# Two of twelve output pairs stored in rows of 4 KB, and a second half-store cut into 92, 4 and 32 partitions

## The chip, the core and the metric

The kernel runs on one NeuronCore of a Trainium2 chip. The core has a matrix engine (TensorE, PE in the profile, with its weight loads as PEld), a vector engine (VectorE, DVE), a scalar engine (ScalarE, ACT), a general engine (GpSimd, POOL), and an engine that here only issues transfers (SyncE, SP). Transfers between the chip's main memory (HBM) and the on-chip memory (SBUF) run on 16 DMA engines. The metric is the device time of one execution in microseconds (us). The kernel before takes 128.76 us, the median of three runs (128.62 to 128.79).

## The reference

Inputs Q, K and V have the shape (8, 12, 512, 64) in float32: 96 heads of 512 tokens with 64 features. For each head:

```
Q_norm = Q / (norm of Q over the 512 tokens)          # a norm per feature
K_norm = K / (norm of K over the 512 tokens)
attn   = einsum('bhnd,bhne->bhde', Q_norm, K_norm)    # 64 x 64, contracted over tokens
attn   = softmax(attn, last axis)
out    = einsum('bhnd,bhde->bhne', V, attn)           # 512 x 64
```

Three inputs of 12.58 MB are read and one output of 12.58 MB is written. Nothing is read twice.

## The kernel before

Four heads make a unit (`HU = 4`), so there are `U = 24` units. Two units make a pair, `S = 12` pairs `s`; two pairs make one of `W = 6` loads of V.

**The way to the attention matrix.** Rows of Q and K come in by DMA (`load_qk`, line 172), are cast to bf16 next to each other (`cast_qk`, 209), and one chain of matmuls per head accumulates all products of features (`grams`, 221). The diagonal gives the norms (`squares`, `sums`, `powers`), the off-diagonal block gives the logits, and `exps` (278) and `normalise` (285) leave `ab[s]`: for each of four head positions a 128 x 128 block-diagonal bf16 matrix that holds the attention of the head of unit 0 and of the head of unit 1.

**The way to the output.** V comes in rows of 32 tokens, 8 KB each (`load_v`, 189), is cast (`cast_v`) and transposed on TensorE (`vtrans`, 295) to `vt[w]` of shape [128, 8 j, 128 x, 4 c]: features of two units on the partitions, and for each row x (16 rows a head) its token 8c + j. `outs` (310) then multiplies. A piece `x` of pair `s` is `(i, k) = divmod(x, 2)`: `i` picks two of four head positions, `k` picks four of eight `j`. Each piece is 8 matmuls: for each `j` and each of two heads, 64 columns of `vt` (16 rows times 4 `c`) are the weights, the 128 columns of `ab` stream through, and the result lands on 64 partitions of the PSUM tile `po` (two buffers). `ocopy` (321) copies `po` to the SBUF tile `so[s, i]` of shape [128, 2 r, 8 j, 64], on ACT or, in the last pairs, on DVE. So a partition of `so[s, i]` holds, for each of the two units `r`, eight neighbouring tokens of one head: 512 floats, which are a run of 2 KB in the output. `sop` (147) has 13 buffers for these tiles (`NB`, 140), so a tile waits for the store of the tile 13 before it.

**The stores.** `store` (198) writes a tile of 512 KB as one DMA of 256 rows of 2 KB (line 207). Two stores are not like that. The store of pair 9, `i = 1` (`FEW`, 122) is four DMAs: its half `r = 0` goes in parts of 92, 4 and 32 partitions (line 204), its half `r = 1` whole (line 205). The last store, of pair 11, `i = 1`, is cut by `j` into two DMAs of 256 rows of 1 KB (planned at 457 and 458), the first of which needs one piece less.

**What sets the order.** Nothing is scheduled by hand or by the framework's scheduler: `Order` (the class at the top) is a small list scheduler that runs while the kernel is being written out. Every step is a `piece` with a cost for each engine it may run on, what it must come after, and a rank; `run` picks the next step, and each engine's instructions stand in that order. The planner also counts PE instructions (`size`, 353; `pause`, 44) to allow for instruction fetches. All DMAs but two (the first K loads, on ACT's queue) are issued by SP, in one queue. SP issues a DMA only when the instructions before it in its queue are through and the data or the buffer is there.

SP's last instructions, in order: fourteen stores of 512 KB (pairs 2 to 9; the fourteenth is pair 9, `i = 0`), the four DMAs of pair 9, `i = 1`, then three stores of 512 KB (pair 10 twice, pair 11 `i = 0`) and two of 256 KB (pair 11, `i = 1`). Below, the stores of pairs 10 and 11 are called the last four stores.

Of the kernel before, what the change touches and what calls it, by code (L numbers as in the profile page):

```python
# [8 lines left out]
F32 = mybir.dt.float32  # L9
# [4 lines left out]
D = 64  # L14
T = 16
HU = 4
J = T // 2
# [85 lines left out]
def kernel(  # L103
# [7 lines left out]
    nc = tc.nc  # L111
# [3 lines left out]
    S = U // 2  # L115
# [4 lines left out]
    HELD, UNTIL = ("lk", 1, 1), ("cq", 0, 1)  # L120
    BOTH = S - 8
    FEW = (S - 3, 1)

# [8 lines left out]

    Of = out.rearrange("b h n d -> (b h n d)").rearrange(
        "(w r e i p x) -> w e i p r x", r=2, e=2, i=2, p=128, x=J * D)

    ctx.enter_context(tc.manual_schedule())

    NB = dict(qk=3, v=3, vb=2, qkb=2, vt=2, so=13, sm=2, ab=4)  # L140
    const = ctx.enter_context(tc.tile_pool(name="const", bufs=1))
    qp = ctx.enter_context(tc.tile_pool(name="qp", bufs=NB["qk"]))
    vp = ctx.enter_context(tc.tile_pool(name="vp", bufs=NB["v"]))
    vbp = ctx.enter_context(tc.tile_pool(name="vbp", bufs=NB["vb"]))
    qkp = ctx.enter_context(tc.tile_pool(name="qkp", bufs=NB["qkb"]))
    vtp = ctx.enter_context(tc.tile_pool(name="vtp", bufs=NB["vt"]))
    sop = ctx.enter_context(tc.tile_pool(name="sop", bufs=NB["so"]))
    small = ctx.enter_context(tc.tile_pool(name="small", bufs=NB["sm"]))
    ps_v = ctx.enter_context(tc.tile_pool(name="ps_v", bufs=1, space=bass.MemoryType.PSUM))
    ps_l = ctx.enter_context(tc.tile_pool(name="ps_l", bufs=1, space=bass.MemoryType.PSUM))  # L150
# [11 lines left out]
    qk32, v32, vb, qkb, gram, scr, kq, n2, r8, kqs, rq, lg, ex, ab, vps, vt, po, so = ({} for _ in range(18))  # L162

    def copy(eng, o, i):
        if eng == "ACT":
            nc.scalar.copy(o, i)  # L166
        elif eng == "DVE":
            nc.vector.tensor_copy(o, i)  # L168
        else:
            nc.gpsimd.tensor_scalar(out=o, in0=i, scalar1=1.0, scalar2=0.0, op0=ALU.mult, op1=ALU.add)  # L170
# [24 lines left out]
        else:  # L195
            nc.sync.dma_start(out=o[:, c], in_=i[:, c])

    def store(s, i, k=None):
        rows = slice(None) if k is None else slice(k * (J // 2), (k + 1) * (J // 2))
        o = Of[s // 2, s % 2, i].rearrange("p r (j d) -> p r j d", d=D)  # L200
        if (s, i) == FEW:

            for a, b in ((0, 92), (92, 96), (96, 128)):
                nc.sync.dma_start(out=o[a:b, 0], in_=so[s, i][a:b, 0])
            nc.sync.dma_start(out=o[:, 1], in_=so[s, i][:, 1])
            return
        nc.sync.dma_start(out=o[:, :, rows], in_=so[s, i][:, :, rows])

    def cast_qk(u, x):
        s, r = divmod(u, 2)  # L210
# [99 lines left out]
    def outs(s, x):  # L310
        i, k = divmod(x, 2)
        w, half = divmod(s, 2)
        po[s, x] = ps_o.tile([128, J // 2, 2, D], F32, name="po")
        for j in range(J // 2):
            for e in range(2):
                h = 2 * i + e
                x16 = slice(16 * (4 * half + h), 16 * (4 * half + h + 1))
                v = vt[w][:, k * (J // 2) + j, x16, :].rearrange("p x c -> p (x c)")
                nc.tensor.matmul(po[s, x][e * D:(e + 1) * D, j].rearrange("p r d -> p (r d)"), v, ab[s][:, h, :])  # L319

    def ocopy(eng, s, x):
        i, k = divmod(x, 2)
        if k == 0:
            so[s, i] = sop.tile([128, 2, J, D], F32, name="so")
        o = so[s, i][:, :, k * (J // 2):(k + 1) * (J // 2)].rearrange("p r j d -> p j r d")
        copy(eng, o, po[s, x])


# [2 lines left out]
    for r in range(2):  # L331
# [7 lines left out]
        name=nc.get_next_instruction_name(), engine=mybir.EngineType.Activation, ins=[], outs=[], act_func_set_id=LN_EXP))  # L339
# [8 lines left out]
    for i in range(NB["ab"]):  # L348
        a = const.tile([128, HU, 2 * D], BF16, name=f"ab{i}")
# [3 lines left out]
    def size(key):  # L353
        if key[0] == "gr" and key[1] >= WIDE:
            return 64
        return 8 if key[0] == "vt" and key[-1] is not None else {"gr": 128, "lg": 8, "vt": 16, "ou": 16}[key[0]]

    plan = Order(size)
    X = 1.29
    R = dict(cq=2.5, gr=2.471, sq=0.756, kq=1, rd=3.457, pw=3.5, sc=1, rq=1.9, lg=5, ex=1.1, nm=2.545, cv=1.165, vt=0.9, vc=1.1, ou=2, oc=0.9)  # L360
    BIAS = dict(sc=-0.6, kq=5, cv=1, vc=-0.3, oc=0.6)
    QK_PACE, V_FROM, V_PACE, ST_LAG = 0.631, 0.0377, 0.7486, 1.5133

    def v_at(v):
        return V_FROM + V_PACE * v / U

    def piece(key, engines, after, behind, rank, fn, *args):
        if key[0] in ("cv", "vc", "oc", "kq", "sc"):
            plan.add(key, engines, after, behind, rank, lambda eng: fn(eng, *args))
        else:  # L370
            plan.add(key, engines, after, behind, rank, lambda eng: fn(*args))

    def back(kind, i, n, *rest):
        return (kind, i - n, *rest) if i - n >= 0 else None
# [5 lines left out]
    def loaded(x, s, r):  # L380
        return ("l" + "qk"[x], s, r if len(parts(s)) == 2 else None)

    last = None
    for s in range(S):
        free = [back("cq", 2 * s + r, 2 * NB["qk"], x) for r in range(2) for x in range(2)]
        for r in parts(s):
            at = QK_PACE * (2 * s + (r or 0)) / U
            for x in range(2):
                key = loaded(x, s, r)
                piece(key, {"DMA": X if r is not None else 2 * X}, free, [last], at, load_qk, s, x, r)  # L390
                last = key
    for u in range(U):
        s, r = divmod(u, 2)
# [17 lines left out]
    def turns(w):  # L411
        return [(q, f) for q in range(4) for f in ((0, 1) if w == W - 1 and q >= TAIL else (None,))]

    last, turned = None, None
    for w in range(W):
        both = 2 * w >= BOTH
        for r in range(2):
            halves = (0, 1) if (w, r) == (W - 1, 1) else (None,)
            n = 2 * w + r - NB["v"]
            for c in halves:  # L420
                free = [("cv", n // 2, n % 2, h) for h in range(2)] if n >= 0 else []
                piece(("lv", w, r, c), {"DMA": X if c is not None else 2 * X}, free, [last], v_at(4 * w + 2 * r + (c or 0)), load_v, w, r, c)
                last = ("lv", w, r, c)
            for c in range(2):
                free = [("vt", w - NB["vb"], *t) for t in turns(w - NB["vb"])] if w >= NB["vb"] else []
                piece(("cv", w, r, c), {"POOL": 1.15, "DVE": (0.72, BIAS["cv"])} if both else {"POOL": 1.15},
                      [("lv", w, r, c if len(halves) == 2 else None)] + free, [("cv", w, r, 0)] if c else [], R["cv"] + 0.01 * (4 * w + 2 * r + c), cast_v, w, r, c)
        for n, (q, f) in enumerate(turns(w)):
            if f is None:
                before = turns(w)[n - 1] if n else turns(w - 1)[-1] if w else None  # L430
                wait = [("vc", w if n else w - 1, *before)] if before else []
            else:
                wait = [("kq", S - 1)] + ([("vc", w, *turns(w)[n - 4])] if n >= 4 and turns(w)[n - 4][1] is not None else [])
# [6 lines left out]
            free = [("ou", 2 * (w - NB["vt"]) + e, x) for e in range(2) for x in range(4)] if w >= NB["vt"] else []  # L440
            piece(("vc", w, q, f), copies, [("vt", w, q, f)] + free, [("vc", w, *turns(w)[n - 1])] if n else [], R["vc"] + 0.02 * w, vcopy, w, q, f)
    for s in range(S):
        for x in range(4):
            i, k = divmod(x, 2)
            n = 4 * s + x - 2
            wait = [("oc", n // 4, n % 4)] if n >= 0 else []
            order = [("ou", s, x - 1) if x else back("ou", s, 1, 3)]
            piece(("ou", s, x), {"PE": 0.5}, [("vc", s // 2, *t) for t in turns(s // 2) if t[0] // 2 == k] + [("nm", s)] + wait, order, R["ou"] + 0.01 * s, outs, s, x)
            n = 2 * s + i - NB["so"]
            free = [("st", n // 2, n % 2)] if k == 0 and n >= 0 else []  # L450
            order = [("oc", s, x - 1) if x else back("oc", s, 1, 3)]
            piece(("oc", s, x), {"ACT": 0.6, "DVE": (0.68, BIAS["oc"])} if s >= BOTH else {"ACT": 0.6}, [("ou", s, x)] + free, order, R["oc"] + 0.01 * s, ocopy, s, x)
        for i in range(2):
            order = [("st", s, 0) if i else back("st", s, 1, 1)]
            if (s, i) == (S - 1, 1):

                piece(("sh", s, i), {"DMA": 0.67}, [("oc", s, 2)], order, v_at(2 * s + i) + ST_LAG, store, s, i, 0)
                piece(("st", s, i), {"DMA": 0.67}, [("oc", s, 3)], [("sh", s, i)], v_at(2 * s + i) + ST_LAG, store, s, i, 1)
            else:
                piece(("st", s, i), {"DMA": X}, [("oc", s, 2 * i), ("oc", s, 2 * i + 1)], order, v_at(2 * s + i) + ST_LAG, store, s, i)  # L460

    ahead = [loaded(x, 0, r) for r in range(2) for x in range(2)]
    held, passed = [], False
# [40 lines left out]
```

## Time and profile before

| what | value |
|---|---|
| median of three runs | 128.76 us (128.62 to 128.79) |
| span of the profiled execution, first to last instruction | 126.98 us |
| the median less this span: what lies around it | 1.78 us |
| DMA: bytes, mean rate | 50.64 MB, 399 GB/s |
| DMA queue 1, share of 16 engines over the span | 96.4% |
| busy share PE, PEld, DVE, ACT, POOL | 61%, 50%, 73%, 57%, 29% |
| last copy of an output tile to SBUF ends | 115.07 us |
| last DMA packet ends | 125.73 us |

The profile is of one execution; its times run from the span's start. The page gives the share of each engine, the span in 40 slices with the DMA rate, the queues, and the issues with their median time from issue to landing. A DMA is cut into packets, here one for each contiguous run in HBM (1, 2, 4 or 8 KB), and on each DMA engine that it uses it ends with a 4-byte packet that counts up a semaphore. So the trace holds, for each DMA, one landing event for each DMA engine that took part, and the DMA has landed when all have come. The windows view gives, for any stretch of the span, the busy time of each engine, the DMA share and the rate. A DMA share a little over 1 is full: records of neighbouring packets overlap by some nanoseconds.

### The profile page before, as it was taken

To read this page: it belongs to the slowest core of one execution; us is meant where nothing else is said; L and a number is where in the kernel's file an instruction comes from. 1 tells how busy PE (TensorE), PEld (TensorE's weight loads), DVE (VectorE), ACT (ScalarE), POOL (GpSimd) and SP (SyncE) were. 2 spreads that over 40 slices of the span, in tenths; PEclk is the share of its full clock that TensorE was granted. 3 is DMA by queue.
4 is the path that set the end of the run, shared out by engine and by line. 5 is a ranking of instruction groups with operands and counts; after the bars stand their busy time and mean duration, and the time that the engine had idled before them with its cause. 6 is when DMAs were issued, how large, how long until landed. Compare 5 with 4: busy or idle time off the path is not lost.

```text
span 127.0 us, 4887 instructions
## 1 busy us (share of the span) xinstructions
PE 77.7 (61%) x2128; PEld 62.9 (50%) x2128; DVE 92.8 (73%) x141; ACT 72.5 (57%) x220; POOL 36.6 (29%) x40
## 2 busy tenths in 40 slices
PE   0065384894844679858594879566797869680000
PEld 0054372773633568647482668445585748460000
DVE  3354749859899899999885898999999799820000
ACT  4000441569877077786692786794829969972000
POOL 4006307300906903033065212213453361200000
PEclk9999999999998555999958967998559995955555
DMA  4999999999999999999999999999999999999993
GB/s 114 415 434 410 430 410 418 417 437 403 425 426 415 410 419 421 405 415 426 430 410 413 415 421 427 412 419 428 401 413 410 403 402 406 401 405 408 405 366 106
DMA packets 15629, 50.64 MB, mean 399 GB/s; under 512 B 1144, under 2 KB 1656, under 8 KB 14200
## 3 DMA queue, kind: packets, MB, share of 16 engines
q1 hardware_dynamic: 15320, 49.29, 96.4%
q10 hardware_dynamic: 288, 1.05, 2.1%
q8 instruction: 16, 0.26, 0.7%
q14 instruction: 5, 0.04, 0.1%
HBM read 37.75 MB, written 12.58 MB: 396 GB/s over the span
## 4 chain that ended last, share of the span: by engine, by line
DVE 39%; DMA 21%; PE 13%; ACT 11%; issue 4%; POOL 2%; DVEq 0%; SPq 0%; POOLq 0%; ACTq 0%
DMA qk<-in_Q_dram 21%; DVE qkb L213 15%; PE gram L233 9%; DVE scr L240 7%; DVE ab L291 6%; ACT vt L166 4%; DVE vb L168 4%; ACT ex L282 3%; ACT so L166 3%; PE vps L302 3%; DVE n L252 2%; DVE vt L168 2%; DVE so L168 2%; PE po L319 1%; ACT kq L166 1%
## 5 line engine op out<-in xcount | busy, mean ns | idle before, releaser
L233 PE MATMUL gram<-qkb 32*128 32x128 bf16 (+1 forms) x1504 | 35.5, 257 | 23.1 <-DVE qkb L213 9.9
L233 PEld LDWEIGHTS <-qkb 32*128 32x128 bf16 (+1 forms) x1504 | 29.9, 114 | 27.7 <-DVE qkb L213 12.7
L213 DVE CAST qkb<-qk 128x1024 bf16<-128x1024 f32 x48 | 36.4, 780 | 8.5 <-DMA qk<-in_Q_dram 6.9
L170 POOL TENSOR_SCALAR vb<-v 128x1024 bf16<-128x1024 f32 x19 | 21.2, 1129 | 45.5 <-DMA v<-in_V_dram 32.0
L166 ACT COPY so<-po 128x512 f32<-128x512 f32 x45 | 25.0, 593 | 5.2 <-PE po L319 5.0
L166 ACT COPY vt<-vps 128x1024 bf16<-128x1024 bf16 (+1 forms) x18 | 17.8, 989 | 17.4 <-PE vps L302 17.3
L302 PE MATMUL vps<-identb,vb 128*128 128x128 bf16 x192 | 20.2, 262 | 5.8 <-POOL vb L170 3.7
L319 PE MATMUL po<-ab,vt 128*64 128x128 bf16 x384 | 19.3, 242 | 5.2 <-issue 2.7
L263 POOL TENSOR_TENSOR kqs<-kq,r 64x512 f32<-64x512 f32 x12 | 14.0, 1164 | 25.8 <-ACT r L259 13.4
L240 DVE SCALAR_TENSOR_TENSOR scr<-gram,eye 64x512 f32<-64x512 f32 x24 | 16.5, 687 | 4.4 <-PE gram L233 4.1
L302 PEld LDWEIGHTS <-vb 128*128 128x128 bf16 x192 | 14.7, 117 | 10.0 <-POOL vb L170 5.1
L319 PEld LDWEIGHTS <-vt 128*64 128x64 bf16 x384 | 13.8, 121 | 9.2 <-issue 4.6
L282 ACT ACTIVATE ex<-lg,rq 128x64 f32<-128x64 f32 x48 | 14.5, 322 | 2.8 <-PE lg L276 2.7
L166 ACT COPY kq<-gram 64x512 f32<-64x512 f32 x12 | 7.0, 581 | 13.5 <-DVE scr L240 13.4
L291 DVE TENSOR_TENSOR ab<-ex,rinv 64x256 bf16<-64x256 f32 x24 | 13.9, 579 | 0.6
L282 ACT ACTIVATION_READ_ACCUMULATOR ex<-lg,rq 128x1 f32 x48 | 10.2, 213 | 0.0
L168 DVE CAST vb<-v 128x1024 bf16<-128x1024 f32 x5 | 7.6, 1527 | 1.2 <-DMA v<-in_V_dram 1.2
L252 DVE TENSOR_REDUCE n<-scr 128x8 f32<-128x512 f32 x12 | 8.1, 679 | 0.1
L276 PE MATMUL lg<-eye,kqs 64*128 64x64 f32 x48 | 6.4, 259 | 2.6 <-issue 1.5
L168 DVE COPY vt<-vps 128x1024 bf16<-128x1024 bf16 (+1 forms) x8 | 7.9, 1019 | 0.1
L276 PEld LDWEIGHTS lg<-eye,kqs 64*128 64x128 f32 x48 | 4.5, 156 | 4.4 <-issue 2.0
L288 DVE RECIPROCAL rinv<-esum 128x4 f32<-128x4 f32 x12 | 2.1, 171 | 2.8 <-ACT ex L282 2.8
(17 smaller groups left out, 16.0 us busy)
## 6 DMA issues: line engine op xcount, KB each, us to landing
v<-in_V_dram SPq DMA_DIRECT2D x11, 1024.0 KB, 17.1
out_dram<-so SPq DMA_DIRECT2D x22, 512.0 KB, 10.2
qk<-in_Q_dram SPq DMA_DIRECT2D x8, 1024.0 KB, 17.4
qk<-in_K_dram SPq DMA_DIRECT2D x8, 1024.0 KB, 17.1
qk<-in_Q_dram SPq DMA_DIRECT2D x8, 512.0 KB, 12.2
qk<-in_K_dram SPq DMA_DIRECT2D x6, 512.0 KB, 12.5
qk<-in_K_dram ACTq DMA_DIRECT2D x2, 512.0 KB, 7.3
v<-in_V_dram SPq DMA_DIRECT2D x2, 512.0 KB
```

What stands on the lines that cost most here:

```text
L166: nc.scalar.copy(o, i)
L168: nc.vector.tensor_copy(o, i)
L170: nc.gpsimd.tensor_scalar(out=o, in0=i, scalar1=1.0, scalar2=0.0, op0=ALU.mult, op1=ALU.add)
L213: nc.vector.tensor_copy(qkb[u][:, :, x * D:(x + 1) * D], qk32[s][:, x, r])
L233: nc.tensor.matmul(gram[s][:, h, r, 0], x, x, start=(t == 0), stop=(t == (T if u < WIDE else J) - 1))
L240: nc.vector.scalar_tensor_tensor(out=scr[s][half], in0=gram[s][half, :, :, 0, half].rearrange("p h r d -> p (h r) d"), scalar=1e-20, in1=e ...
L263: (nc.vector if eng == "DVE" else nc.gpsimd).tensor_tensor(out=kqs[s][HI], in0=kq[s][HI], in1=r8[s][HI, :, None].to_broadcast([D, 2 * HU, ...
L276: nc.tensor.transpose(l[:, h, :], kqs[s][HI, 2 * h:2 * h + 2].rearrange("p r d -> p (r d)"), eye2[HI])
L282: nc.scalar.activation(e[:, h, :], lg[s][:, h, :], AF.Exp, scale=rq[s][:, h:h + 1], accum_out=z[:, h:h + 1])
L291: nc.vector.tensor_tensor(out=a[half, :, half], in0=e[half], in1=ri[half, :, None].to_broadcast([D, HU, D]), op=ALU.mult,)
L302: nc.tensor.transpose(ps[:, c, n, :], vb[w][:, J * c + j].rearrange("p r d -> p (r d)"), identb)
L319: nc.tensor.matmul(po[s, x][e * D:(e + 1) * D, j].rearrange("p r d -> p (r d)"), v, ab[s][:, h, :])
```

## The change

Three things change, and the plan is computed anew with them.

1. Pairs 10 and 11 (`s >= LONG`, `LONG = S - 2`) are multiplied and stored in another layout. In `outs`, `i` now picks two of the four `c` (every second column), and all four heads go side by side: 16 matmuls a piece in place of 8, each with 32 weight columns in place of 64, each landing on 32 partitions. The 128 streamed columns stay. A partition then holds, for each unit, 16 neighbouring tokens of one head, a run of 4 KB. One tile `so[s]` of [128, 2, 16, 64] a pair (pool `slp`, two buffers) takes all four pieces. Its two stores are the two units, each 128 rows of 4 KB, and each waits for all four pieces.
2. The store of pair 9, `i = 1` goes in parts of 92, 4 and 32 partitions for both halves `r`: six DMAs in place of four.
3. The last store is no longer cut in two. `sop` has 12 buffers in place of 13, and the planner's costs and counts follow (0.9 for a piece of 16 matmuls, 32 instructions, a store at 1.23).

```
-    NB = dict(qk=3, v=3, vb=2, qkb=2, vt=2, so=13, sm=2, ab=4)
+    NB = dict(qk=3, v=3, vb=2, qkb=2, vt=2, so=12, sm=2, ab=4)
+    Ol = out.rearrange("b h n d -> (b h n d)").rearrange("(w r e p x) -> w e p r x", r=2, e=2, p=128, x=T * D)
+    slp = ctx.enter_context(tc.tile_pool(name="slp", bufs=S - LONG))
...
-    def store(s, i, k=None):
-        rows = slice(None) if k is None else slice(k * (J // 2), (k + 1) * (J // 2))
-        o = Of[s // 2, s % 2, i].rearrange("p r (j d) -> p r j d", d=D)
-        if (s, i) == FEW:
-
-            for a, b in ((0, 92), (92, 96), (96, 128)):
-                nc.sync.dma_start(out=o[a:b, 0], in_=so[s, i][a:b, 0])
-            nc.sync.dma_start(out=o[:, 1], in_=so[s, i][:, 1])
-            return
-        nc.sync.dma_start(out=o[:, :, rows], in_=so[s, i][:, :, rows])
+    def store(s, i):
+        if s >= LONG:
+            o, t = Ol[s // 2, s % 2][:, i], so[s][:, i].rearrange("p t d -> p (t d)")
...
+        else:
+            o, t = Of[s // 2, s % 2, i], so[s, i].rearrange("p r j d -> p r (j d)")
+            if (s, i) == FEW:
+                for r in range(2):
+                    for a, b in ((0, 92), (92, 96), (96, 128)):
+                        nc.sync.dma_start(out=o[a:b, r], in_=t[a:b, r])
+                return
+        nc.sync.dma_start(out=o, in_=t)
...
-            for e in range(2):
-                h = 2 * i + e
+            for e in range(HU if s >= LONG else 2):
+                h = e if s >= LONG else 2 * i + e
...
-                v = vt[w][:, k * (J // 2) + j, x16, :].rearrange("p x c -> p (x c)")
-                nc.tensor.matmul(po[s, x][e * D:(e + 1) * D, j].rearrange("p r d -> p (r d)"), v, ab[s][:, h, :])
+                v = vt[w][:, k * (J // 2) + j, x16, slice(i, None, 2) if s >= LONG else slice(None)].rearrange("p x c -> p (x c)")
+                n = 32 if s >= LONG else D
+                nc.tensor.matmul(po[s, x][e * n:(e + 1) * n, j].rearrange("p r d -> p (r d)"), v, ab[s][:, h, :])
...
-            if (s, i) == (S - 1, 1):
-
-                piece(("sh", s, i), {"DMA": 0.67}, [("oc", s, 2)], order, v_at(2 * s + i) + ST_LAG, store, s, i, 0)
-                piece(("st", s, i), {"DMA": 0.67}, [("oc", s, 3)], [("sh", s, i)], v_at(2 * s + i) + ST_LAG, store, s, i, 1)
-            else:
-                piece(("st", s, i), {"DMA": X}, [("oc", s, 2 * i), ("oc", s, 2 * i + 1)], order, v_at(2 * s + i) + ST_LAG, store, s, i)
+            done = range(4) if s >= LONG else (2 * i, 2 * i + 1)
+            piece(("st", s, i), {"DMA": X - (0.06 if s >= LONG else 0)}, [("oc", s, x) for x in done], order, v_at(2 * s + i) + ST_LAG, store, s, i)
```

The new plan moves little. SP's queue is the same up to the 92-partition part; then come 92, 4, 32, 92, 4, 32 partitions and four stores of 128 rows of 4 KB. PE's order is the same, with 64 matmuls and 64 weight loads more in the pieces of pairs 10 and 11. ACT makes two output copies of pair 7 after the four exponentials that stood behind them, and one of pair 8 after two small activations that stood behind it; one copy of pair 10 goes from DVE to ACT. POOL's order is the same.

More of the change, by code (lines that the diff above doesn't have):

```diff
@@ L122 @@
     FEW = (S - 3, 1)
+    LONG = S - 2
     Qu = Q.rearrange("b h (p t) d -> (b h p) (t d)", t=T).rearrange("(w r e p) x -> w e p r x", r=2, e=2, p=128)
@@ L196, in load_v @@
             nc.sync.dma_start(out=o[:, c], in_=i[:, c])
-    def store(s, i, k=None):
-        rows = slice(None) if k is None else slice(k * (J // 2), (k + 1) * (J // 2))
-        o = Of[s // 2, s % 2, i].rearrange("p r (j d) -> p r j d", d=D)
-        if (s, i) == FEW:
-            for a, b in ((0, 92), (92, 96), (96, 128)):
-                nc.sync.dma_start(out=o[a:b, 0], in_=so[s, i][a:b, 0])
-            nc.sync.dma_start(out=o[:, 1], in_=so[s, i][:, 1])
-            return
-        nc.sync.dma_start(out=o[:, :, rows], in_=so[s, i][:, :, rows])
+    def store(s, i):
+        if s >= LONG:
+            o, t = Ol[s // 2, s % 2][:, i], so[s][:, i].rearrange("p t d -> p (t d)")
+            if s == FEW[0]:
+                for a, b in ((0, 92), (92, 96), (96, 128)):
+                    nc.sync.dma_start(out=o[a:b], in_=t[a:b])
+                return
[3 more added lines that the diff above has]
+                for r in range(2):
+                    for a, b in ((0, 92), (92, 96), (96, 128)):
+                        nc.sync.dma_start(out=o[a:b, r], in_=t[a:b, r])
+                return
+        nc.sync.dma_start(out=o, in_=t)
     def cast_qk(u, x):
@@ L314, in outs @@
         for j in range(J // 2):
-            for e in range(2):
-                h = 2 * i + e
+            for e in range(HU if s >= LONG else 2):
+                h = e if s >= LONG else 2 * i + e
                 x16 = slice(16 * (4 * half + h), 16 * (4 * half + h + 1))
-                v = vt[w][:, k * (J // 2) + j, x16, :].rearrange("p x c -> p (x c)")
-                nc.tensor.matmul(po[s, x][e * D:(e + 1) * D, j].rearrange("p r d -> p (r d)"), v, ab[s][:, h, :])
+                v = vt[w][:, k * (J // 2) + j, x16, slice(i, None, 2) if s >= LONG else slice(None)].rearrange("p x c -> p (x c)")
+                n = 32 if s >= LONG else D
+                nc.tensor.matmul(po[s, x][e * n:(e + 1) * n, j].rearrange("p r d -> p (r d)"), v, ab[s][:, h, :])
     def ocopy(eng, s, x):
         i, k = divmod(x, 2)
-        if k == 0:
+        if s >= LONG and x == 0:
+            so[s] = slp.tile([128, 2, T, D], F32, name="sl")
+        elif s < LONG and k == 0:
             so[s, i] = sop.tile([128, 2, J, D], F32, name="so")
-        o = so[s, i][:, :, k * (J // 2):(k + 1) * (J // 2)].rearrange("p r j d -> p j r d")
+        o, at = (so[s], i * J) if s >= LONG else (so[s, i], 0)
+        o = o[:, :, at + k * (J // 2):at + (k + 1) * (J // 2)].rearrange("p r j d -> p j r d")
         copy(eng, o, po[s, x])
@@ L355, in size @@
             return 64
-        return 8 if key[0] == "vt" and key[-1] is not None else {"gr": 128, "lg": 8, "vt": 16, "ou": 16}[key[0]]
+        return 8 if key[0] == "vt" and key[-1] is not None else {"gr": 128, "lg": 8, "vt": 16, "ou": 32 if key[0] == "ou" and key[1] >= LONG else 16}[key[0]]
     plan = Order(size)
@@ L447 @@
             order = [("ou", s, x - 1) if x else back("ou", s, 1, 3)]
-            piece(("ou", s, x), {"PE": 0.5}, [("vc", s // 2, *t) for t in turns(s // 2) if t[0] // 2 == k] + [("nm", s)] + wait, order, R["ou"] + 0.01 * s, outs, s, x)
+            piece(("ou", s, x), {"PE": 0.9 if s >= LONG else 0.5}, [("vc", s // 2, *t) for t in turns(s // 2) if t[0] // 2 == k] + [("nm", s)] + wait, order, R["ou"] + 0.01 * s, outs, s, x)
             n = 2 * s + i - NB["so"]
-            free = [("st", n // 2, n % 2)] if k == 0 and n >= 0 else []
+            free = [("st", n // 2, n % 2)] if k == 0 and n >= 0 and s < LONG else []
             order = [("oc", s, x - 1) if x else back("oc", s, 1, 3)]
```

## The prediction

> **What bounds the kernel.** I read the page first. Its 40 slices show the DMA engines full from the second slice to the last but one; DVE, the busiest compute engine, has 73%. So the sum of transfers sets the length, if they never run dry. The windows view of the end shows how they stop (columns that matter: DMA share and GB/s, last two; PE clock before them):
>
> ```profile
> DMA  4999999999999999999999999999999999999993
> GB/s 114 415 434 410 430 410 418 417 437 403 425 426 415 410 419 421 405 415 426 430 410 413 415 421 427 412 419 428 401 413 410 403 402 406 401 405 408 405 366 106
> DMA packets 15629, 50.64 MB, mean 399 GB/s; under 512 B 1144, under 2 KB 1656, under 8 KB 14200
> ```
> ```profile
> 112.00:116.00 4.00, 2.24 (x32) 1.77 (x32) 0.00 (x0) 2.59 (x5) 0.00 (x0) 0.50 1.05 406
> ...
> 120.00:122.00 2.00, 0.00 (x0) 0.00 (x0) 0.00 (x0) 0.00 (x0) 0.00 (x0) 0.50 1.06 407
> 122.00:122.50 0.50, 0.00 (x0) 0.00 (x0) 0.00 (x0) 0.00 (x0) 0.00 (x0) 0.50 0.98 371
> 122.50:123.00 0.50, 0.00 (x0) 0.00 (x0) 0.00 (x0) 0.00 (x0) 0.00 (x0) 0.50 0.87 336
> ...
> 124.50:125.00 0.50, 0.00 (x0) 0.00 (x0) 0.00 (x0) 0.00 (x0) 0.00 (x0) 0.50 0.65 229
> 125.00:125.25 0.25, 0.00 (x0) 0.00 (x0) 0.00 (x0) 0.00 (x0) 0.00 (x0) 0.50 0.17 57
> 125.25:125.50 0.25, 0.00 (x0) 0.00 (x0) 0.00 (x0) 0.00 (x0) 0.00 (x0) 0.50 0.07 25
> 125.50:126.00 0.50, 0.00 (x0) 0.00 (x0) 0.00 (x0) 0.00 (x0) 0.00 (x0) 0.50 0.03 10
> ```
>
> All computing ends at 115; then 16 full DMA engines drain what SP has queued. They do not stop together: from 122.0 some are idle, at 122.5 to 123.0 a share of 0.87 of 1.05 is 13 engines, and after 125.25 one of sixteen (0.07) works alone until 125.73. The kernel ends with its slowest DMA engine, so two things count: the work in the queue, and how it is spread.
>
> **How the work is spread.** Each store's landing is up to sixteen semaphore events, one an engine. From the trace's events, in us:
>
> ```
> pair 9, i=0, whole    116.44 116.52 116.85 117.00 117.10 117.44 118.09 118.09 119.11 119.21 119.25 119.29 119.32 119.34 119.51 119.52
> 92 partitions, r=0    118.70 118.95 119.30 119.94
>  4 partitions, r=0    118.88 119.12 119.48 120.12
> 32 partitions, r=0    116.65 116.69 117.18 118.28 119.06 119.30 119.32 119.39 119.44 119.47 119.50 119.55 119.67 119.68 119.69 120.30
> last store, 2nd half  122.48 122.69 123.03 124.00 124.81 125.07 125.13 125.25 125.28 125.31 125.34 125.37 125.41 125.53 125.54 126.05
> ```
>
> Eight engines run 2.7 to 3.1 us behind the first, eight are ahead. The parts of 92 and of 4 partitions run on four engines only. The page agrees: section 6 lists 73 DMAs; 71 x 16 + 2 x 4 = 1144, its count of packets under 512 B. So the four do 23 + 1 + 2 = 26 rows of that half and the other twelve 2, where a whole half gives 8 to each. In the trace's packets a 2 KB row takes 84 ns and the next starts 80 ns after it (16 x 2048 B / 80 ns = 410 GB/s, the rows above). 23 rows are 1.85 us, so the four are those that landed the whole store at 118.70 - 1.85 = 116.85, 117.10, 117.44 and 118.09. They follow on: 118.70, 118.88, 119.06 for the first of them, 119.94, 120.12, 120.30 for the last. After it nothing is uneven, and the last rows show the same four at 124.81, 125.07, 125.41 and 126.05: 5.75 us behind their 32-partition parts each. So **one of the four is already the last engine of all**, 0.51 us behind the last of the twelve (125.54).
>
> **The change, part by part.**
>
> *The second half in parts.* Each of the four gets 26 rows and 3 completion packets (6 ns each by the packets) where it had 8 and 1: 18 x 80 + 2 x 6 = +1.45 us. Each of the twelve gets 2 rows for 8: -0.48 us. The slowest is one of the four, so +1.45.
>
> *Rows of 4 KB.* An engine's share of the last four stores (in five DMAs) was 3 x (16 x 80 + 6) + 2 x (16 x 42.5 + 6) = 5.23 us (1 KB rows: 42.5 ns from start to start). Now it is 4 x (8 x 155 + 6) = 4.98 us. The 155 ns is the pitch of the loads' 4 KB rows (packets of 159 ns); a store with such rows is not in this trace. Bounds: two 2 KB rows, 160 ns, for the least gain, which leaves 0.09 us; half of an 8 KB row's 305 ns for the most, 0.33 us. I take 155, its own size: **-0.25 us**, on all sixteen.
>
> *The last store whole.* That gain is in the sum. It now waits for all four pieces in place of two, and so do the others of the last four; see the cover below.
>
> *Two DMAs more on SP.* SP's row of issues has one every 1.28 us from 92.8 on, paced by landings: eight DMA semaphores go round, so a store is issued when the eighth before it has landed (the 92-partition part at 110.63, after a landing at 110.57). The six parts take the slots at 110.6, 111.8, 113.1, 114.4, 115.75 and 117.05; the four last stores get 118.3, 119.6, then, once 92 and 4 have landed, 120.05 and about 120.5. The slowest of the four ends its 32-partition packets of the first half at 119.85 (landed 120.30), so it reaches the first of them at 119.85 + 2.10 = 121.95 and the third at 124.4, so nothing is short there. The eight late engines reach the first at about 119.5, an issue is 1.0 us from its first packet (first issue 0.74, first packet 1.75), so they may idle some tenths, and stay ahead of the four.
>
> The Trainium skill bears on this ("DMA: Bandwidth & Descriptors", Measured, and Rules for kernel authors): it gives about 2.0 us fixed a DMA (for a software-made one) and says that under 64 KB one pays mostly overhead. By that the two added DMAs would cost up to 4 us. The trace disagrees: the 8 KB part landed 0.18 us after the 92-partition part on each of its engines, and the share stays at 1.05 around it, as the queue is full. I take nothing.
>
> *PE, ACT, buffers.* 64 matmuls and weight loads come on top, after 109.7. In the stretch 112 to 116, at half clock, 32 matmuls take 2.24 us, 70 ns each; a 32-column form is not in the trace, so from no gain of time by narrower weights (70) down to half of it (35, the same piece time as now): the eight pieces take 4.5 to 9.0 us. With 12 buffers, pair 8's second tile waits for the store that lands at 102.81, where its first copy ran at 100.9; ACT's exponentials behind it come 0.6 us later, so PE starts at 110.3 and ends by 119.3, the last copy (0.59) by 119.9. The third of the last four stores, whose slot is 120.05, just doesn't wait. The cover: the slowest DMA engine needs it at 124.4, so computing could be 3 us later still before the end moves.
>
> *More instructions.* Queue 8 shows 16 instruction fetches of 16 KB; two times eight engines each fell 1.3 to 1.6 us behind the rest, in the landings, where one came. 128 more PE instructions may bring a seventeenth. On one of the eight late ones it costs nothing: they will be 2.4 us ahead of the last (126.05 + 1.45 against 125.54 - 0.48).
>
> **Sum.** +1.45 - 0.25 = +1.20 us on the last DMA engine: the last packet at 126.93 for 125.73, the span 128.18 for 126.98. With the 1.78 us around it, 129.96, that is the median 128.76 + 1.20. With the bounds of the 4 KB rows 129.88 to 130.12. The lag of the slowest of the four grew by 0.6 us between 104 and 113 (1.02 to 1.65 behind the first). Without that, before would end with the twelve (125.54) and after with the four at 125.41 + 1.20: +1.07. So 129.8 to 130.2 for this case.
>
> **Rivals.**
>
> *Other engines take the second half's parts, or the four are really further ahead* (faster). If the second 92 and 4 fell on four early engines of the twelve (116.44 to 118.09), these would end at most at 124.00 + 1.20 = 125.20, and the former four gain 0.48 + 0.25: 128.03. The same comes out if, in an execution without the profiler, the four lead by 1.9 us more than here. For it: the early ones have the room. Against: 92 and 4 of the first half hit the same four, and nothing in the queue shows a choice. The page named above (Why a DMA increments its semaphore by 16) says that such a transfer takes the lowest-numbered engines, always the same; that speaks against it too. Chance 0.14.
>
> *The four lead by about 1.2 us more than here, so that overload and relief cancel*: 128.6 to 129.0. Chance 0.08.
>
> *Late data* (slower): PE's last pieces, held by a fetch or a wait beyond the cover, move the last two stores. It decides from an issue at 123.4; a fetch's spacing of 6 us on top of 119.9 would be 125.9, 2.5 us past that: 132.5. Against: the fetch before lies 6 us and more back. Chance 0.04.
>
> **How the numbers follow.** Four overloaded engines 0.74, at 129.96. A measurement can tell about 0.2% (0.26 us) from no change. Slower 0.74 + 0.04 = 0.78, same 0.08, faster 0.14. The range takes the forecast's own bounds and reaches to the cancelling case: 128.6 to 130.4, which leaves out the two ends, 0.18.
>
> **What would show it.** Right: over the last microsecond the share falls to four engines (0.25) and then to one; the two 92-partition parts land on the same four; last stores' packets at 159 ns; computing over by 120. Wrong on the spread: all engines stop within half a microsecond. Wrong on the cover: a stretch before 122 with a share well under 1.

## The result, and the profile after

The changed kernel takes 130.34 us, the median of four runs (130.18 to 130.54), against 128.72 us (128.62 to 128.79) before: 1.62 us more. The ratio on record is 1.0129, 95% interval 1.0116 to 1.0143; it is taken from all runs, here and below, and is not exactly the quotient of the two medians (1.0126). The forecast was 129.96 us. The profiled execution has a span of 128.42 us, 1.43 us more than before, and its last DMA packet ends at 127.09 us, 1.36 us later.

From the page after: the packets, the two queues that matter, and the issues of the stores (KB each, then the median us from issue to landing).

```profile
DMA  3999999999999999999999999999999999999791
GB/s 114 410 433 413 427 410 419 420 431 406 434 424 412 407 424 419 401 413 431 429 411 409 422 416 421 424 422 410 407 413 406 405 401 405 401 405 344 285 419 79
DMA packets 14854, 50.66 MB, mean 394 GB/s; under 512 B 1136, under 2 KB 1136, under 8 KB 13424
...
q8 instruction: 17, 0.28, 0.8%
...
out_dram<-so SPq DMA_DIRECT2D x19, 512.0 KB, 11.5
...
out_dram<-sl SPq DMA_DIRECT2D x4, 512.0 KB, 3.9
```

Of before, for comparison:

```profile
q8 instruction: 16, 0.26, 0.7%
...
out_dram<-so SPq DMA_DIRECT2D x22, 512.0 KB, 10.2
```

Two slices near the end now hold 344 and 285 GB/s where before held 408 and 405, and the last slice but one is full again. The packets fell from 15629 to 14854, above all because the stores of pairs 10 and 11 now have 512 rows where they had 1280. Queue 8 has a seventeenth instruction fetch. The last four stores land 3.9 us after their issue, where a store took 10.2 us before: they no longer stand in a full queue.

The windows view of the same stretch (last three columns: PE clock, DMA share, GB/s):

```profile
112.00:116.00 4.00, 3.06 (x96) 1.97 (x95) 0.58 (x2) 3.72 (x7) 0.00 (x0) 0.70 1.05 405
116.00:118.00 2.00, 0.00 (x0) 0.00 (x0) 0.00 (x0) 0.15 (x1) 0.00 (x0) 0.50 0.89 339
118.00:119.00 1.00, 0.00 (x0) 0.00 (x0) 0.00 (x0) 0.00 (x0) 0.00 (x0) 0.50 0.83 317
119.00:120.00 1.00, 0.00 (x0) 0.00 (x0) 0.00 (x0) 0.00 (x0) 0.00 (x0) 0.50 0.61 205
120.00:121.00 1.00, 0.00 (x0) 0.00 (x0) 0.00 (x0) 0.00 (x0) 0.00 (x0) 0.50 0.58 234
121.00:122.00 1.00, 0.00 (x0) 0.00 (x0) 0.00 (x0) 0.00 (x0) 0.00 (x0) 0.50 1.04 424
...
125.50:126.00 0.50, 0.00 (x0) 0.00 (x0) 0.00 (x0) 0.00 (x0) 0.00 (x0) 0.50 0.49 197
126.00:126.50 0.50, 0.00 (x0) 0.00 (x0) 0.00 (x0) 0.00 (x0) 0.00 (x0) 0.50 0.12 49
126.50:127.00 0.50, 0.00 (x0) 0.00 (x0) 0.00 (x0) 0.00 (x0) 0.00 (x0) 0.50 0.06 25
```

There are two things to see. At the end, from 126.0, a share of 0.12 is two of sixteen engines, then one: the overload. But before that, from 116 to 121, engines are idle: a share of about 0.6 where 1.05 is full, between 119 and 121, is nine engines at work and seven idle on average. The waits of SP's queue say for what (us in total, times, longest):

```profile
SPq L215 <- DMA out_dram<-so: 8.5, 12, 0.9
SPq L213 <- DMA out_dram<-so: 7.1, 6, 2.6
```

Line 213 issues the six parts, and one of them waited 2.6 us for an older store's landing. By SP's instructions the parts went out at 110.74, 111.98, 113.26, 114.54, 115.83 and 118.72, the last four stores at 119.80, 121.00, 121.46 and 121.91. The sixth part was held until the store of pair 8, i = 0, had landed on its last engine, at 118.70. Fifteen engines had landed it by 117.1; the sixteenth was busy with the seventeenth fetch, which queue 8's packet shows from 116.69 for 0.95 us. In the landing events one late engine goes from 3.3 to 4.9 us behind the first at this store; why it loses 1.6 us by a packet of 0.95 us is not shown. The next two issues waited for the same engine: 119.80 follows its landing at 119.74, and 121.00 the one at 120.99.

The landings that answer to those shown of before:

```
92 partitions, r=0    118.71 119.01 119.48 120.08
92 partitions, r=1    120.81 121.12 121.58 122.18
32 partitions, r=1, last one on the slowest of the four   122.56
last store            126.00 126.03 126.03 126.05 126.05 126.06 126.06 126.08 126.09 126.09 126.11 126.16 126.24 126.35 126.81 127.41
```

The same spacing in both 92-partition rows, 2.10 us apart, shows that the same four engines took both. By their steps from the first of the last four stores (122.30, 122.61, 123.07, 123.67) they end at 126.05, 126.35, 126.81 and 127.41. Of the other twelve, eleven end together at 126.00 to 126.16, because they had stood idle for the same late issues; the twelfth, at 126.24, is the engine of the fetch, which those issues had waited for.

### The profile page after: what moved, and what is told of

It reads as the page before. It is cut to its first block, busy times and chain, and to the rows that moved or that the text cites. A ratio compares the mean times of both kernels' runs of the same rounds, so it can differ in the third digit from the quotient of the medians.

```text
span 128.4 us, 5010 instructions
## 1 busy us (share of the span) xinstructions
PE 78.0 (61%) x2192; PEld 63.0 (49%) x2192; DVE 92.5 (72%) x140; ACT 73.0 (57%) x221; POOL 36.4 (28%) x40
## 2 busy tenths in 40 slices
DMA packets 14854, 50.66 MB, mean 394 GB/s; under 512 B 1136, under 2 KB 1136, under 8 KB 13424
## 3 DMA queue, kind: packets, MB, share of 16 engines
q10 hardware_dynamic: 288, 1.05, 2.1%
## 4 chain that ended last, share of the span: by engine, by line
DVE 30%; DMA 20%; PE 19%; ACT 14%; issue 7%; SPq 0%; DVEq 0%; ACTq 0%
DMA qk<-in_Q_dram 20%; DVE qkb L221 14%; PE gram L241 13%; DVE scr L248 7%; DVE ab L299 5%; ACT ex L290 4%; PE po L328 3%; ACT vt L169 3%; ACT sl L169 3%; PE vps L310 2%; ACT so L169 2%; DVE n L260 1%; ACT kq L169 1%; DVE vb L171 1%; PE lg L284 1%
## 5 line engine op out<-in xcount | busy, mean ns | idle before, releaser
L241 PE MATMUL gram<-qkb 32*128 32x128 bf16 (+1 forms) x1504 | 37.6, 262 | 23.8 <-DVE qkb L221 8.6
L241 PEld LDWEIGHTS <-qkb 32*128 32x128 bf16 (+1 forms) x1504 | 31.4, 117 | 28.8 <-DVE qkb L221 11.2
L221 DVE CAST qkb<-qk 128x1024 bf16<-128x1024 f32 x48 | 39.0, 836 | 8.0 <-DMA qk<-in_Q_dram 6.2
L169 ACT COPY so<-po 128x512 f32<-128x512 f32 x38 | 21.2, 592 | 7.6 <-PE po L328 6.0
L328 PE MATMUL po<-ab,vt 128*64 128x128 bf16 (+1 forms) x448 | 20.5, 243 | 7.2 <-issue 2.6
L310 PE MATMUL vps<-identb,vb 128*128 128x128 bf16 x192 | 17.8, 243 | 4.4 <-POOL vb L173 1.8
L328 PEld LDWEIGHTS <-vt 128*64 128x64 bf16 (+1 forms) x448 | 14.0, 116 | 12.0 <-issue 6.7
L310 PEld LDWEIGHTS <-vb 128*128 128x128 bf16 x192 | 13.3, 109 | 7.7 <-issue 3.1
L290 ACT ACTIVATION_READ_ACCUMULATOR ex<-lg,rq 128x1 f32 x48 | 10.2, 212 | 0.0
L171 DVE CAST vb<-v 128x1024 bf16<-128x1024 f32 x5 | 5.0, 998 | 0.1
L169 ACT COPY sl<-po 128x512 f32<-128x512 f32 x8 | 4.5, 596 | 0.3
```

Of the source, the lines that this page charges most:

```text
L221: nc.vector.tensor_copy(qkb[u][:, :, x * D:(x + 1) * D], qk32[s][:, x, r])
L241: nc.tensor.matmul(gram[s][:, h, r, 0], x, x, start=(t == 0), stop=(t == (T if u < WIDE else J) - 1))
L290: nc.scalar.activation(e[:, h, :], lg[s][:, h, :], AF.Exp, scale=rq[s][:, h:h + 1], accum_out=z[:, h:h + 1])
L310: nc.tensor.transpose(ps[:, c, n, :], vb[w][:, J * c + j].rearrange("p r d -> p (r d)"), identb)
L328: nc.tensor.matmul(po[s, x][e * n:(e + 1) * n, j].rearrange("p r d -> p (r d)"), v, ab[s][:, h, :])
```

## The experiments

Two theories stood after the result, and both could hold at once. **O**: the rows on four engines set the end, as forecast. **F**: the seventeenth fetch sets it, by the engine that it holds up and by SP's wait for that engine. The first four runs pull them apart; run 5 completes the picture, and the rest look at the gain that was to be had. Runs 1 to 4 were timed beside the kernel before on one chip (its median there 128.67 us), runs 5 to 8 on another (128.64 us); each ratio is to the kernel before of its own group.

**1. `long_one_half`**: as changed, but the second half whole.

```
-                for r in range(2):
-                    for a, b in ((0, 92), (92, 96), (96, 128)):
-                        nc.sync.dma_start(out=o[a:b, r], in_=t[a:b, r])
+                for a, b in ((0, 92), (92, 96), (96, 128)):
+                    nc.sync.dma_start(out=o[a:b, 0], in_=t[a:b, 0])
+                nc.sync.dma_start(out=o[:, 1], in_=t[:, 1])
                 return
```

> The changed kernel with the second half of pair 9's store whole again (one DMA of 128 rows), the rest as changed, with its 128 additional PE instructions. Theory O (the time is set by the rows that the two narrow parts of each half put on four DMA engines; the seventeenth instruction fetch is covered): the four lose 1.45 us of rows and end at 127.09 - 1.45 = 125.64, so 130.3 - 1.45 = 128.9 us or, against before, about the same. Theory F (the seventeenth fetch of 16 KB, which in the changed kernel's trace runs from 116.69 and puts the store of pair 8, i = 0, 1.6 us back on one engine, sets the end by itself): that engine has 0.17 + 0.65 + 4.98 us left after its landing of pair 9, i = 0 (120.99, packets some 0.4 earlier) and ends near 126.4, so about 129.5 us. Both give a gain over the changed kernel; they differ by 0.6 us.

Measured: 129.35 us against 128.67 before, ratio 1.0048 (1.0033 to 1.0064). So the second half in parts costs about 1.0 us of the 1.62, and something is left. The end of its windows view:

```profile
124.00:125.00 1.00, 0.00 (x0) 0.00 (x0) 0.00 (x0) 0.00 (x0) 0.00 (x0) 0.50 0.58 238
125.00:125.50 0.50, 0.00 (x0) 0.00 (x0) 0.00 (x0) 0.00 (x0) 0.00 (x0) 0.50 0.14 57
125.50:126.00 0.50, 0.00 (x0) 0.00 (x0) 0.00 (x0) 0.00 (x0) 0.00 (x0) 0.50 0.06 25
126.00:126.50 0.50, 0.00 (x0) 0.00 (x0) 0.00 (x0) 0.00 (x0) 0.00 (x0) 0.50 0.04 16
```

One engine works alone for over half a microsecond, until 126.38. It is not one of the four: the slowest of those lands the last store at 125.88, this one at 126.72. It is the engine that was 3.1 us behind the first at pair 7's last store and 4.6 us at pair 8's first. Theory F's figure for its end was 126.4. Here O alone fails.

**2. `more_matmuls`**: the kernel before, each matmul of the pieces of pairs 10 and 11 issued twice into the same place.

```
-                nc.tensor.matmul(po[s, x][e * D:(e + 1) * D, j].rearrange("p r d -> p (r d)"), v, ab[s][:, h, :])
+                for _ in range(2 if s >= S - 2 else 1):
+                    nc.tensor.matmul(po[s, x][e * D:(e + 1) * D, j].rearrange("p r d -> p (r d)"), v, ab[s][:, h, :])
```

> The kernel before with every matmul of the output pieces of pairs 10 and 11 issued twice into the same place (the second writes the same numbers), so 64 matmuls and 64 weight loads more, as in the change; all DMAs as before. Theory O: PE has room, the four engines keep their rows: 128.7 us, same. Theory F: queue 8 shows a seventeenth fetch after 115, one of the late engines falls 1.3 to 1.6 us further back, and the end moves by 0.9 us to about 129.7.

Measured: 129.60 us against 128.67, ratio 1.0064 (1.0049 to 1.0079). Not a byte more is stored, and PE is idle after 116, yet 0.9 us are lost. From its page and windows:

```profile
q8 instruction: 17, 0.28, 0.8%
```
```profile
116.00:118.00 2.00, 0.00 (x0) 0.00 (x0) 0.00 (x0) 0.43 (x1) 0.00 (x0) 1.00 1.05 398
118.00:120.00 2.00, 0.00 (x0) 0.00 (x0) 0.00 (x0) 0.00 (x0) 0.00 (x0) 1.00 0.94 364
...
125.50:126.00 0.50, 0.00 (x0) 0.00 (x0) 0.00 (x0) 0.00 (x0) 0.00 (x0) 0.50 0.09 33
126.00:126.50 0.50, 0.00 (x0) 0.00 (x0) 0.00 (x0) 0.00 (x0) 0.00 (x0) 0.50 0.07 25
```

The fetch comes at 116.53, the share is thin after it, and one engine is last, until 126.53. This is F by itself. The Trainium skill ("Runtime: NRT & Kernel Launch", Instruction fetch mechanics) calls the cost of crossing a 16 KiB boundary "one DMA tail-bump, mostly hidden". PE indeed lost nothing by this fetch, as its last matmul had ended at 115.8; the cost is on the other side, on the DMA engine that carries the 16 KB, and in this kernel, bound by its slowest DMA engine, it is 0.9 us.

**3. `both_halves_only`**: the kernel before with both halves in parts, and nothing else.

```
-            for a, b in ((0, 92), (92, 96), (96, 128)):
-                nc.sync.dma_start(out=o[a:b, 0], in_=so[s, i][a:b, 0])
-            nc.sync.dma_start(out=o[:, 1], in_=so[s, i][:, 1])
+            for r in range(2):
+                for a, b in ((0, 92), (92, 96), (96, 128)):
+                    nc.sync.dma_start(out=o[a:b, r], in_=so[s, i][a:b, r])
```

> The kernel before with both halves of pair 9's i = 1 store in parts of 92, 4 and 32 partitions; layout, buffers and the last store as before, no additional PE instruction. Theory O: the slowest of the four engines gets 18 rows of 80 ns and 2 completions more, +1.45 us, 130.2 us, sixteen fetches on queue 8 and no thin stretch before 120. Theory F: without a seventeenth fetch little is lost: 128.3 to 128.9 us.

Measured: 130.38 us against 128.67, ratio 1.0129 (1.0112 to 1.0146): as much as the whole change loses, by this edit alone. Its page has 16 fetches, and its windows end with four engines:

```profile
118.00:119.00 1.00, 0.00 (x0) 0.00 (x0) 0.00 (x0) 0.00 (x0) 0.00 (x0) 0.50 0.82 313
119.00:120.00 1.00, 0.00 (x0) 0.00 (x0) 0.00 (x0) 0.00 (x0) 0.00 (x0) 0.50 0.96 371
...
125.00:125.50 0.50, 0.00 (x0) 0.00 (x0) 0.00 (x0) 0.00 (x0) 0.00 (x0) 0.50 0.26 94
125.50:126.00 0.50, 0.00 (x0) 0.00 (x0) 0.00 (x0) 0.00 (x0) 0.00 (x0) 0.50 0.24 84
126.00:126.50 0.50, 0.00 (x0) 0.00 (x0) 0.00 (x0) 0.00 (x0) 0.00 (x0) 0.50 0.13 45
126.50:127.00 0.50, 0.00 (x0) 0.00 (x0) 0.00 (x0) 0.00 (x0) 0.00 (x0) 0.50 0.06 25
```

From its landing of the first 92 partitions to its last landing, the slowest of the four needs 7.57 us (119.73 to 127.30), where it needed 6.11 before (119.94 to 126.05): 1.46 us more, for 1.45 expected.

Against what was expected here, there is a thin stretch before 120 with no fetch in sight (0.82 at 118). Early engines idle there: each of the six parts takes a slot of eight, so SP has fewer bytes ahead. It is shorter than in the changed kernel, and the twelve still land their last rows by 125.11, well ahead of the four.

**4. `after_fewer_matmuls`**: as changed, with 64 matmuls fewer; the products of units 20 and 21 are summed over half of their tokens.

```
-        for t in range(T if u < WIDE else J):
+        steps = J if u >= WIDE or u in (20, 21) else T
+        for t in range(steps):
...
-                nc.tensor.matmul(gram[s][:, h, r, 0], x, x, start=(t == 0), stop=(t == (T if u < WIDE else J) - 1))
+                nc.tensor.matmul(gram[s][:, h, r, 0], x, x, start=(t == 0), stop=(t == steps - 1))
```

> The changed kernel with the products of units 20 and 21 summed over half of their tokens only (8 steps for 16), so 64 matmuls and 64 weight loads fewer, as many PE instructions as before; the layout of the stores and the six parts stay. Theory O: sixteen fetches, no thin stretch at 116 to 120, and yet the four engines end as late: 130.1 to 130.4 us. Theory F: the loss goes with the fetch: under 129.3 us.

Measured: 130.24 us against 128.67, ratio 1.0117 (1.0102 to 1.0132), with 16 fetches:

```profile
q8 instruction: 16, 0.26, 0.7%
```
```profile
116.00:118.00 2.00, 0.00 (x0) 0.00 (x0) 0.00 (x0) 0.04 (x1) 0.00 (x0) 0.50 0.91 352
118.00:119.00 1.00, 0.00 (x0) 0.00 (x0) 0.00 (x0) 0.00 (x0) 0.00 (x0) 0.50 0.83 320
119.00:120.00 1.00, 0.00 (x0) 0.00 (x0) 0.00 (x0) 0.00 (x0) 0.00 (x0) 0.50 0.96 377
...
126.00:126.50 0.50, 0.00 (x0) 0.00 (x0) 0.00 (x0) 0.00 (x0) 0.00 (x0) 0.50 0.10 41
126.50:127.00 0.50, 0.00 (x0) 0.00 (x0) 0.00 (x0) 0.00 (x0) 0.00 (x0) 0.50 0.06 25
```

The fetch is gone, the loss is not. Its last packet ends at 127.09, to the hundredth where the changed kernel's does, though its last four stores are issued from 118.38 and not from 119.80. Theory O for the changed kernel. As in run 3, and against what was expected, the share is thin at 116 to 120 without a fetch; yet the twelve land their last rows by 124.90, 1.3 us earlier than in the changed kernel.

**5. `one_half_fewer`**: runs 1 and 4 together: one half in parts, 64 matmuls fewer.

> Rows of 4 KB and the last store whole, only one half of pair 9's store in parts, and the products of units 20 and 21 summed over half of their tokens only, so as many PE instructions as before. Both causes of loss are gone; what is left is the shorter tail. Both theories: an engine's share of the last four stores is 4.98 us for 5.23, -0.25 us, 128.4 us against 128.67. If rows of 4 KB gain nothing in a store, only the two halves joined count: 128.6.

Measured: 128.52 us against 128.64, ratio 0.9991 (0.9982 to 1.0). With it the square of two causes is full (ratios to the kernel before; all four with rows of 4 KB):

```
                     16 fetches    17 fetches
one half in parts      0.9991        1.0048
both halves            1.0117        1.0129
```

Each cause costs by itself, 0.6% and 1.3%. Together they cost no more, as far as can be told, than the larger alone (1.0129 and 1.0117 lie inside each other's intervals): they end on different engines, and the end is a maximum.

**6. `last_whole`**: the kernel before, the last store as one DMA.

```
-            if (s, i) == (S - 1, 1):
-
-                piece(("sh", s, i), {"DMA": 0.67}, [("oc", s, 2)], order, v_at(2 * s + i) + ST_LAG, store, s, i, 0)
-                piece(("st", s, i), {"DMA": 0.67}, [("oc", s, 3)], [("sh", s, i)], v_at(2 * s + i) + ST_LAG, store, s, i, 1)
-            else:
-                piece(("st", s, i), {"DMA": X}, [("oc", s, 2 * i), ("oc", s, 2 * i + 1)], order, v_at(2 * s + i) + ST_LAG, store, s, i)
+            piece(("st", s, i), {"DMA": X}, [("oc", s, 2 * i), ("oc", s, 2 * i + 1)], order, v_at(2 * s + i) + ST_LAG, store, s, i)
```

> The kernel before with the last store as one DMA of 256 rows of 2 KB in place of two of 256 rows of 1 KB; nothing else. Theory of rows: 16 x 80 + 6 = 1.29 us on each engine for 2 x (16 x 42.5 + 6) = 1.37 us, -0.09 us: 128.6 us, same within what can be told. Rival: it waits for one piece more; but computing ends at 115 and it is issued after 119, so nothing.

Measured: 128.43 us against 128.64, ratio 0.9986 (0.9977 to 0.9996). A small gain clear of nothing. In landings, the slowest engine needs from the second half of pair 9's store (120.91) to its end 5.13 us here (126.04), 4.98 in run 5 (125.89), and 5.22 before (120.83 to 126.05): the sizes that the rows of 2 and 4 KB were given, -0.09 and -0.24. In the medians runs 5 and 6 can't be told apart.

**7. `last_whole_76`**: run 6 with parts of 76, 4 and 48 partitions.

```
-            for a, b in ((0, 92), (92, 96), (96, 128)):
+            for a, b in ((0, 76), (76, 80), (80, 128)):
```

> last_whole with the first half of pair 9's store in parts of 76, 4 and 48 partitions in place of 92, 4 and 32: the four engines do 19 + 1 + 3 = 23 rows for 26, the twelve 3 for 2. Theory O: in the trace of before the slowest of the four ended 0.51 us behind the slowest of the twelve, so -0.24 us for the end from the one and +0.08 on the other: 128.67 - 0.09 - 0.24 = 128.35 us, faster than both. If the four are not the last in most runs, +0.08 instead: 128.65.

Measured: 128.42 us against 128.64, ratio 0.9984 (0.9975 to 0.9993), the fastest, but by 0.01 us over run 6. In the trace the move is there: the last store lands at 125.66 for 126.04, and its last engines stop nearly together, nine of sixteen landing within the last 0.5 us (four of sixteen in run 6):

```profile
124.00:124.50 0.50, 0.00 (x0) 0.00 (x0) 0.00 (x0) 0.00 (x0) 0.00 (x0) 0.50 0.70 270
124.50:125.00 0.50, 0.00 (x0) 0.00 (x0) 0.00 (x0) 0.00 (x0) 0.00 (x0) 0.50 0.61 238
125.00:125.50 0.50, 0.00 (x0) 0.00 (x0) 0.00 (x0) 0.00 (x0) 0.00 (x0) 0.50 0.16 57
125.50:126.00 0.50, 0.00 (x0) 0.00 (x0) 0.00 (x0) 0.00 (x0) 0.00 (x0) 0.50 0.00 0
```

But run 6's ten times fall into two groups, five at 128.30 to 128.39 and four at 128.64 to 128.69, one at 128.47 between them, and its profiled one (128.66) is of the upper, while run 7's (128.29) is of its fastest. In the lower group the slowest of the four seems to be less late, so that there was nothing to take from it. That is argued from the times, not shown.

**8. `no_split`**: the kernel before with no store in parts.

```
-        if (s, i) == FEW:
+        if False:
```

> The kernel before with pair 9's i = 1 store as one whole DMA like the others. Theory O from the trace of before: the four would end at 126.05 - 1.45 = 124.6, the slowest of the twelve at 125.54 + 0.48 = 126.02, so the same as before within 0.1 us, 128.65 us. If parts on four engines paid before, it is slower, up to 129.1.

Measured: 128.91 us against 128.64, ratio 1.0016 (1.0007 to 1.0025). Slower than expected: one half in parts is worth 0.27 us, where the trace of before gave nothing. In its trace the twelve are last, as expected, but the last of them lands at 126.16, 0.14 us later than expected. Another 0.12 us is that the trace of before, on which the expectation rests, was a run at 128.76 us, above the median of 128.64. Whether the four are less late in its faster runs is not shown.

## Why the prediction was right, point by point

**The bound and the spread**: right. The end is the slowest DMA engine, and it is one of the four that take the parts of 92 and 4. In the changed trace these took both halves' parts.

**The second half in parts, +1.45 us**: right for the four. From the 32 partitions of the first half to those of the second the slowest needs 2.13 us by landings (120.43 to 122.56) for 2.10. Run 3 shows that the edit alone makes the loss. For the twelve the step failed: they were to end 0.73 us earlier, at 124.81, and landed up to 1.43 us later than that (126.24). That is the fetch: without it, in run 4, they land by 124.90. The prediction saw that they may idle, "some tenths", and took the slots of SP without the fetch.

**Rows of 4 KB, -0.25 us**: right in the traces (4.98 us in run 5 for 5.22 before, the last store whole included). The result cannot show this term by itself. In medians run 5 gains 0.12 us, at the edge of what can be told, and run 6, with the last store whole and rows of 2 KB, gains no less.

**The last store whole**: no wait came of it. Copies end at 116.2, SP issues from 119.8.

**PE, ACT, buffers**: nothing here reached the end, as forecast, and PE was cheaper than its bounds. Here is what the pieces of pairs 10 and 11 took, and one piece of before in the last line:

```profile
110.43 0.63 PE L328 MATMUL po<-ab,vt 128*32 128x128 bf16 x32 [0.36 <-DVE ab L299]
112.02 0.89 PE L328 MATMUL po<-ab,vt 128*32 128x128 bf16 x32 [0.96 <-ACT sl L169]
113.11 2.41 PE L328 MATMUL po<-ab,vt 128*32 128x128 bf16 x64 [0.20 <-ACT sl L169]
```
```profile
109.72 0.64 PE L319 MATMUL po<-ab,vt 128*64 128x128 bf16 x16 [0.59 <-DVE ab L291]
```

At full clock, 32 matmuls with 32 columns take 0.63 us where 16 with 64 columns took 0.64 us in the kernel before. Both times include the end of the last matmul (about 0.2 us); by the starts in the traces, one follows the other after 14 ns where it was 28. At half clock it is 27 ns for 53. So the 70 ns that the prediction read at half clock, as busy time by count, was too long, and its lower bound of 35 ns still above what came. From the third piece on, the pieces waited for ACT's copies, 4.80 us for eight.

**Two DMAs more on SP**: right that they cost no fixed time on the end, and right on the slots where no fetch holds them (run 4 issues the last four stores at 118.38, 119.61, 120.15 and 120.53, for 118.3, 119.6, 120.05 and 120.5 forecast); wrong that the slots keep the engines busy. The six small parts leave fewer bytes in SP's eight slots, so the early ones among the twelve run dry even in run 4 (a share of 0.83 at 118), and one late engine then holds the issue for all. With the fetch seven engines on average stood idle for two microseconds. That this did not show in the end is luck as much as foresight: the four were later still. (The DMAs that the prediction counts, 73, are those of the DMA view; the page's section 6 lists its eight largest groups, 67 of them. The skill's page has the 2.0 us under "Anatomy of one DMA", not under "Measured".)

**More instructions**: the seventeenth fetch came, on a late engine, 1.6 us, and "costs nothing" held only under the cover of the four: run 4 puts it at 0.1 us there, which can't be told from nothing, and runs 1 (against run 5) and 2 at 0.7 and 0.9 us without that cover. The prediction gave it the right engine and no price for the case that the cover is gone.

**The size**: +1.20 forecast; +1.43 between the two profiled spans, of which 0.14 is that the slowest of the four was that much later already at the first half's 92 partitions (120.08 for 119.94), 0.02 its way from there, and 0.07 what follows the last packet (1.33 us for 1.25). The medians differ by 1.62. The profiled execution of before was above its kernel's median and that after (130.2) below. By medians the second half in parts alone costs 1.71 us (run 3) for the 1.45 forecast, and the rows of 4 KB with the last store whole gain 0.12 (run 5) for 0.25: these two sizes are what the sum missed. The traces have both at the forecast size (+1.46 and -0.24), so the rest may be how late the four come to these stores: the slowest lands its first 92 partitions between 119.73 (run 3, in the fastest execution of that kernel) and 120.08 in the profiled executions. That this makes the difference of the medians is argued, not shown, and why it varies stays open. The time, 130.34, lies 0.06 us under the upper end of the range.

**The signs**: the two 92-partition parts hit the same four, the last stores' packets take 159 ns and computing is over at 116.2, as said for the case of being right. In the last microsecond the share fell to two engines (0.12) and then to one, not to four first, as the late issues had brought the twelve close. A stretch before 122 with a share well under 1 was the sign of being wrong on the cover, and it came (0.58), though not by late data: SP's slots and the fetch made it.

**The rivals**: the fast one fell (the second parts hit the same four), the cancelling one too; the late data did not come.

## What to carry to other kernels

Where the DMA engines are full to the end, count the work of each engine and not of all: sixteen landing events a transfer give the lag of every engine, and an edit that loads some of them pays only until they are the last. A few instructions more on an engine with time to spare are not free there: a fetch of 16 KB on one DMA engine moved the end by 0.9 us (run 2), as that engine was late. And when two causes end on different engines, undo both in turn and together, or the smaller will be called harmless.

## What the runs showed that was not expected

- A store cut into six small DMAs starved engines that ran ahead: SP had eight in flight, six of them with 512 KB in all, and the DMA share fell to 0.82 at 118 to 119 with 16 fetches (run 3), and to 0.58 at 120 to 121 with the seventeenth (the changed kernel).
- Matmuls with 32 weight columns followed each other every 14 ns at full clock, half of the 28 ns with 64 columns, with the same 128 streamed columns and four heads side by side.
- Nine of ten executions of one kernel (run 6) fell into two groups about 0.35 us apart; why is not shown.
